# State tiles two items ahead, sums between the first products, and scratch in the other PSUM banks

## The chip, the cores and the metric

The kernel runs on one core of one Trainium2 chip. The metric is the device time of one execution in microseconds (us). All arithmetic is in float32; the large products use the float32r form of TensorE's input, in three matmuls each (hi x hi, hi x lo, lo x hi).

Names used below: PE is TensorE (matmul), DVE is VectorE, ACT is ScalarE, POOL is GpSimd, and SP is SyncE, which here only issues DMAs. POOL issues DMAs too. Each engine works through its own queue in order, and so do the two queues that issue DMAs.

## The reference

One layer of a hybrid decoder, for a prompt of 1024 tokens and, with the same weights, one step of 8 samples. Cut to what matters:

```python
shift, scale, gate = split(silu(c) @ w_ada + b_ada, 3)
h = rmsnorm(x, g_norm) * (1 + scale) + shift
p = h @ w_in                      # 2048 -> 8200: q k v o z, gates i f, u v_cm z_cm
h_ml = mLSTM heads (4 heads of 256), chunkwise, with a state C of 256x256 per head
h_cm = u * spatial_mix(layernorm(gelu(v_cm))) * silu(z_cm)
out = concat([h_ml, h_cm]) @ w_out
y = rmsnorm(x + gate * out, g_final)
```

For the samples the state comes in and goes out: `C_new = decay * C + g_end * v k^T`, and `C q` enters the head's output. There are 8 x 4 states of 256 x 256. The outputs are y for both groups, the new states, and the normalised rows of the second branch.

## The kernel before

The kernel is traced by a planner that puts instructions into each engine's queue. It is free to move an instruction ahead of others that were written before it when it holds that one to be ready sooner; `late(...)` forbids that for one instruction: it stays behind everything already written on its engine. Tiles come from pools with a fixed number of slots for each tag; a new tile waits until the slot's last reader is done.

**Stages.** First x is loaded and its row norms are taken (lines 1346 to 1365). The squares are summed through `accum_out`; their element results go to a PSUM tile `tr` that nobody reads. PSUM has two tags of four banks: `pp` (`psb()`, general use) and `px` (`psx()`, the large products). Then `ada_first` computes shift and scale of the first 512 features (L197 loads, L201 matmuls, L204 a copy).

`sub_phase` computes p = h @ w_in with a seven-product scheme (Strassen's), in three passes over the inner dimension (`SUBS`): 32 sections of 256 output columns each, and for each section seven products (`product`, L387) of a weight combination (`sums` L360, `split` L371/L372) with one of seven combinations of h. These seven combinations for each block of 256 features are made by `combos`: for each an ACT cast (L310) and a DVE subtraction (L311), and four more DVE operations (L316, L317, L323, L330), 11 DVE operations a block. `combos` is a generator of seven steps. The first pass takes blocks 0 and 1. Before it, for each of the two, `h_block` makes h (transposes L276, ACT L277, gate product L283) in the one tile `hf` of pool `pre` (one slot), and `combos` then runs to its end. `bg` is the background of a pass: one of its steps after each product. In the first pass it begins with `ada_pair` for blocks 2 to 4 (weight loads L174 on SP, three slots; matmuls L178), whose copy takes a scratch tile of tag `s2` (three slots). `combos` takes three such tiles a block, and `sample_two` (L422) one for each pair of sections, stored through SP.

After the third pass and the streams that compute the heads, `out_proj` multiplies by w_out: two halves of the tokens, four column groups each, 16 tiles k of w_out in a group. For each k, `take` loads tiles of w_out through SP five ahead (lines 887 to 889) and has ACT cast (L870) and DVE subtract (L871) three ahead; then come 12 matmuls (L908, L909, L910). From the second group on, the sample's work `back_b` runs between them: after 14 of the 16 tiles of a group one step, after every second of these one more, which is 21 steps a group.

**The sample's steps.** `s_sum` and `s_ml1` prepare sums, gates and scaled rows (18 steps). Then come the 16 state items `s_state(b, hp)`: POOL loads a state tile `Ct` (L1190, 128 x 1024, 512 KB) and two tiles of q and k rows spread over all partitions (`g2`, L1194, 256 KB each); ACT scales the tile (L1198, twice), DVE multiplies it with q (L1202, four times) and adds the new part (L1207, four times); POOL stores it (L1210). `Ct` has three slots (`CTB`), `g2` four in all. In each round of two steps one item is loaded, the item before it is computed, and the item before that is stored. All of these are `late`.

After that `s_cm` and `s_ml2` finish both branches of the sample with small transfers, and `s_out` multiplies by w_out again: 32 loads of 512 KB on POOL into the same `Ct` slots, issued two ahead (L1262), each with four matmuls (L1294), and a final norm.

Of the kernel before, what the change touches and what calls it, by code (L numbers as in the profile page):

```python
# [8 lines left out]
F32 = mybir.dt.float32  # L9
# [5 lines left out]
P = 128  # L15
# [3 lines left out]
NB = 8  # L19
# [14 lines left out]
def tile_decoder_step(  # L34
# [26 lines left out]
    def nm(s):  # L61
        uid[0] += 1
        return f"{s}{uid[0]}"
# [25 lines left out]
    def psb():  # L89
        return pp.tile([P, 512], F32, tag="pp", name=nm("pp_"))  # L90
# [335 lines left out]
        A.copy(e, ps)  # L426
        to_dram(sa.sub, psd[:, sa.n * 256:sa.n * 256 + 512], e)

    def sub_phase(sub, at, bg, turn=None):
        secs = {}  # L430

        def get(n):
            if n < len(SECS) and n not in secs:
                secs[n] = Seven(sub, n)

        AHEAD = 2
        get(0)
        get(1)
        secs[0].sums()
        for m in range(AHEAD):  # L440
            secs[0].split(m)
        last = len(SECS) - 1
        for n in range(len(SECS)):
            s = secs[n]
            s.load_co()
            if n == last and turn is not None:
                for _ in bg:
                    pass
                bg = turn()
            for m in range(7):  # L450
                if m == 3 and n + 1 < len(SECS):
                    secs[n + 1].sums()
                g = m + AHEAD
                if g < 7:
                    s.split(g)
                elif n + 1 < len(SECS):
                    secs[n + 1].split(g - 7)
                if m == 1 and n % 2 == 0:
                    sample_two(s, secs[n + 1])
                s.product(m, at)  # L460
                for _ in range(1 if sub < 2 else (0, 2, 0, 2, 0, 0, 3)[m]):
                    next(bg, None)
            s.store()
            if sub == len(SUBS) - 1 and n:
                avail.add(SECS[n - 1])
            get(n + 2)
            del secs[n]
        avail.update(SECS if sub == len(SUBS) - 1 else [])
        if turn is not None:
            for _ in bg:  # L470
                pass
# [738 lines left out]
        late(G.dma_start(nC_s[0, b, 2 * hp_:2 * hp_ + 2].rearrange("h (a p) d -> p (h a) d", p=P), Ct))  # L1210
        yield

    CTB = 3

    def s_ml2(so):
        d, v, cq = sv["d"], sv["v"], sv["cq"]
# [29 lines left out]
    def s_out():  # L1246
        ts_ = []
        for _ in range(4):
            yield
        for n in range(4):  # L1250
            t = g2([NB, 512])
            late(G.dma_start(t, hc_d[:, n * 512:n * 512 + 512]))
            ts_.append(t)
        rows = [(n, hf, kq) for n in range(4) for hf in range(2) for kq in range(4)]
        raws = {}

        def get(i):
            if i < len(rows) and i not in raws:
                n, hf, kq = rows[i]
                raws[i] = pl["wp"].tile([P, 4, 256], F32, tag="Ct", name=nm("Ct"), bufs=CTB)  # L1260
                c0 = n * 512 + hf * 256
                late(G.dma_start(raws[i], wout[:, 4 * kq:4 * kq + 4, c0:c0 + 256]))  # L1262

        for i in range(CTB - 1):
            get(i)
        for _ in range(4):
            yield
        pt = psb()
        for n in range(4):
            for i in range(4):  # L1270
                kt = 4 * n + i
                late(T.transpose(pt[:, kt * NB:kt * NB + NB], ts_[n][:, i * P:i * P + P], ident[0:NB, 0:NB]))
        V.tensor_copy(hs[:, :, 0:NB], pt[:, 0:KT * NB].rearrange("p (k b) -> p k b", b=NB))
        yield
        part = sm([NB, 4])
        ys = []
        pend = None

        def row(n, e, xl, gt):
            p2 = psb()  # L1280
            late(T.matmul(p2[0:16, :], sel9, e, start=True, stop=True))
            y = pl["gp"].tile([NB, 512], F32, tag="ym"[n // 2], name=nm("ys"), bufs=2)
            V.tensor_tensor(out=y, in0=p2[0:NB, :], in1=gt, op=ALU.mult)
            V.tensor_tensor(out=y, in0=y, in1=xl, op=ALU.add)
            t = g2([NB, 512])
            A.activation(t, y, AF.Square, accum_out=part[:, n:n + 1])
            ys.append(y)

        for i, (n, hf, kq) in enumerate(rows):
            if (hf, kq) == (0, 0):  # L1290
                ps = psb()
            raw = raws.pop(i)
            for g in range(4):
                late(T.matmul(ps[32 * g:32 * g + 32, hf * 256:hf * 256 + 256], hs[:, 4 * kq + g, :], raw[:, g, :],  # L1294
                              start=(kq == 0), stop=(kq == 3), tile_position=(0, 32 * g)))
            get(i + CTB - 1)
            if (hf, kq) == (0, 1) and pend is not None:
                row(*pend)
                pend = None
            if (hf, kq) == (1, 3):  # L1300
                e = g2([P, 512])
                A.copy(e, ps)
                xl = pl["wp"].tile([NB, 512], F32, tag="gt", name=nm("xl"), bufs=4)
                late(G.dma_start(xl, x_sample[:, 0, n * 512:n * 512 + 512]))
                gt = pl["wp"].tile([NB, 512], F32, tag="gt", name=nm("gt"), bufs=4)
                late(G.dma_start(gt, gate_d[0:NB, n * 512:n * 512 + 512]))
                pend = (n, e, xl, gt)
            yield
        yield
        row(*pend)  # L1310
        ssq, rs = sm([NB, 1]), sm([NB, 1])
        V.tensor_reduce(out=ssq, in_=part, axis=AX.X, op=ALU.add)
        G.tensor_scalar(out=rs, in0=ssq, scalar1=1.0 / DM, scalar2=EPS, op0=ALU.mult, op1=ALU.add)
        G.tensor_tensor(out=rs, in0=rs, in1=mhalf[0:NB, 0:1], op=ALU.pow)
        for n in range(4):
            gt = pl["wp"].tile([NB, 512], F32, tag="gt", name=nm("gt"), bufs=4)
            late(G.dma_start(gt, gfin[:, n * 512:n * 512 + 512].partition_broadcast(NB)))
            yield
            V.scalar_tensor_tensor(out=ys[n], in0=ys[n], scalar=rs, in1=gt, op0=ALU.mult, op1=ALU.mult)
            G.dma_start(y_sample[:, 0, n * 512:n * 512 + 512], ys[n])  # L1320


    def back_b():
        so, decb = sv["so"]
        yield from s_sum()
        yield from s_ml1(so)
        g0 = g1 = iter(())
        for b in range(NB + 1):
            for hp_ in range(2):
                g2_ = s_state(b, hp_, decb) if b < NB else iter(())  # L1330
                next(g2_, None)
                yield
                next(g1, None)
                next(g1, None)
                next(g0, None)
                g0, g1 = g1, g2_
                yield
        yield from s_cm()
        yield from s_ml2(so)
        yield from s_out()  # L1340
# [5 lines left out]
    for tt in range(8):  # L1346
        part_ = sm([P, 4])
        xr = [pl["s1"].tile([P, 2, 512], F32, tag="asS", name=nm("xr"), bufs=7) for _ in range(2)]
        for n in range(4):
            if n % 2 == 0:  # L1350
                S.dma_start(xr[n // 2].rearrange("p a b -> p (a b)"), xp[:, tt, n * 512:n * 512 + 1024])
            tr = psb()
            xv = xr[n // 2][:, n % 2, :]
            if n % 2 == 0:
                A.activation(tr, xv, AF.Square, accum_out=part_[:, n:n + 1])
            else:
                V.scalar_tensor_tensor(out=tr, in0=xv, scalar=1.0, in1=xv, op0=ALU.mult, op1=ALU.mult, accum_out=part_[:, n:n + 1])
# [12 lines left out]
    def hf_tile(pool="pre"):  # L1370
        t = pl[pool].tile([P, 4, 512], F32, tag="hf", name=nm("hf"), bufs=1)
        return t, [t[:, i, :] for i in range(4)]

    sets = [("as", "A"), ("as", "B"), ("as", "C"), ("s1", "S")]
    at = {b: [] for b in range(8)}
    ada_first()
    for blk in range(2):
        hf = hf_tile()[1]
        for _ in h_block(blk, lambda tt: xk[tt // 2][:, tt % 2, blk * 256:blk * 256 + 256], [0, 1], hf):
            pass  # L1380
        for _ in combos(at[blk], sets[blk], hf, V):
            pass

    nxt = {}

# [32 lines left out]
    def turn_b():  # L1418
        close_pool("adp")
        open_pool("hf2", "right")  # L1420
        t, hf = hf_tile("hf2")
        S.dma_start(t.rearrange("p a b -> p (a b)"), hf7)
        g6, g7 = combos(at[6], sets[2], nxt[6][1], V), combos(at[7], sets[0], hf, V)
        for _ in range(7):
            next(g6)
            next(g7)
            yield

    sub_phase(0, [at[0], at[1]], bg_a(), turn_a)
    sub_phase(1, [at[2], at[3], at[4]], bg_b(), turn_b)  # L1430
    for name in ("hf2", "pre", "co"):
        close_pool(name)
# [20 lines left out]
    open_pool("w2", "right")  # L1453

    def turn():
        close_pool("co")
        close_pool("c2")
        open_pool("ya", "left")
        open_pool("wp", "left")

    out_proj(streams, turn, back_b())
    for name in ("wp", "ya", "rp", "gp", "w2", "hx"):
        close_pool(name)
# [29 lines left out]
```

## Time and profile before

| | us |
|---|---|
| median of 3 runs | 2180.51 |
| lowest and highest | 2178.35, 2185.18 |
| profiled execution | 2184.66 |
| its span, from first to last instruction | 2182.9 |

| engine | busy us | share of the span |
|---|---|---|
| PE (matmul) | 2010.4 | 92% |
| PE weight load | 1511.3 | 69% |
| DVE | 1344.2 | 62% |
| ACT | 856.4 | 39% |
| POOL | 321.0 | 15% |

The core moved 402.68 MB by DMA, 184 GB/s over the span; the mean granted clock of PE was 0.969 of full speed. In the chain of work that ended last, the largest DMA part is the store of state tiles (out_dram<-Ct, 3% of the span).

How to read it: matmuls are pipelined and their ends are modelled, so a busy PE can still be short of its peak; the granted clock tells how fast it was let run. A share of busy time is a mean over stages with different limits, which is why the stretches are looked at one by one. Releasers of waits are inferred from semaphore events.

### The profile page before, as it was taken

What the parts mean: (1) busy time and instruction counts of PE and PEld (TensorE: products, weight loads), DVE (VectorE), ACT (ScalarE), POOL (GpSimd) and SP (SyncE); (2) the same over time, 40 slices, a digit from 0 to 9 for tenths busy, and PEclk for the clock granted to TensorE, in tenths of its full rate; (3) what the DMA queues carried; (4) which work ended last, traced back from release to release, by engine and by line L of the source; (5) the groups of instructions that cost most, each with busy time, mean ns of one, the idle gap of its engine ahead of it and who ended that gap; (6) DMA issues with size and microseconds to landing.
All of it is one profiled execution on the core that took longest, in us unless ns stands there. A gap on an engine that the chain in (4) does not pass through costs nothing. (4 is left out here: it accounts for less than half of the span.)

```text
span 2182.9 us, 29261 instructions
## 1 busy us (share of the span) xinstructions
PE 2010.4 (92%) x10175; PEld 1511.3 (69%) x10175; DVE 1344.2 (62%) x2775; ACT 856.4 (39%) x1771; POOL 321.0 (15%) x499
## 2 busy tenths in 40 slices
PE   2999999999999999998899999999998996767997
PEld 1467777766766777777688788788786775554476
DVE  3568777755644555558667767767766655453264
ACT  2435434433422233334346456456455433231132
POOL 1000000011111111111211111111110132244300
PEclk9999999999999999999999999999999998878999
DMA  8685444488799676665676776776877877867843
GB/s 282 205 281 182 174 160 172 175 231 214 179 247 241 124 136 127 129 128 114 141 176 138 166 194 138 181 181 138 181 165 174 261 209 207 237 203 249 275 132 134
DMA packets 227396, 402.68 MB, mean 184 GB/s; under 512 B 20784, under 2 KB 136192, under 8 KB 226984
## 3 DMA queue, kind: packets, MB, share of 16 engines
q1 hardware_dynamic: 188560, 280.92, 40.4%
q0 software_dynamic: 38688, 119.89, 28.7%
q8 instruction: 80, 1.31, 0.3%
q14 instruction: 68, 0.56, 0.1%
HBM read 259.56 MB, written 141.19 MB: 184 GB/s over the span
## 5 line engine op out<-in xcount | busy, mean ns | idle before, releaser
L387 PE MATMUL px<-as,hi 128*128 128x512 f32 x3584 | 1147.5, 401 | 17.6 <-DVE pu L390 8.3
L387 PEld LDWEIGHTS px<-as,hi 128*128 128x128 f32 x3584 | 660.6, 189 | 214.9 <-issue 25.9
L387 PE MATMUL px<-as,lo 128*128 128x512 f32 x1792 | 707.5, 396 | 2.4 <-DVE lo L372 2.2
L387 PEld LDWEIGHTS px<-as,lo 128*128 128x128 f32 x1792 | 338.7, 189 | 82.6 <-DVE lo L372 4.4
L371 ACT CAST hi<-t 128x384 fp32r<-128x384 f32 (+1 forms) x384 | 182.5, 477 | 397.9 <-PE px L387 390.7
L372 DVE TENSOR_TENSOR lo<-t,hi 128x384 fp32r<-128x384 f32 (+1 forms) x384 | 195.4, 509 | 161.5 <-ACT hi L371 161.3
L371 ACT CAST hi<-raw 128x384 fp32r<-128x384 f32 (+1 forms) x288 | 137.3, 477 | 370.4 <-PE px L387 336.9
L908 PE MATMUL px<-whi,hx 128*128 128x512 f32 x512 | 212.8, 418 | 31.7 <-DVE yacc L993 22.2
L910 PE MATMUL px<-wlo,hx 128*128 128x512 f32 x512 | 212.0, 419 | 29.8 <-DVE wlo L871 29.8
L336 POOL DMA_DIRECT2D spool<-co x128 | 112.1, 876 | 809.0 <-DVE co L390 567.5
L909 PE MATMUL px<-whi,hx 128*128 128x512 f32 x512 | 210.5, 412 | 1.1 <-DVE hx L902 1.1
L372 DVE TENSOR_TENSOR lo<-raw,hi 128x384 fp32r<-128x384 f32 (+1 forms) x288 | 146.5, 509 | 50.8 <-ACT hi L371 50.3
L908 PEld LDWEIGHTS px<-whi,hx 128*128 128x128 f32 x512 | 102.2, 200 | 63.4 <-issue 18.0
L910 PEld LDWEIGHTS px<-wlo,hx 128*128 128x128 f32 x512 | 103.0, 202 | 61.0 <-DVE wlo L871 35.1
L870 ACT CAST whi<-raw 128x512 fp32r<-128x512 f32 x128 | 77.1, 617 | 172.0 <-PE px L909 132.8
L390 DVE TENSOR_TENSOR co<-pa,px 128x512 f32<-128x512 f32 x192 | 129.1, 683 | 24.8 <-PE px L387 24.5
L871 DVE TENSOR_TENSOR wlo<-raw,whi 128x512 fp32r<-128x512 f32 x128 | 85.1, 686 | 85.3 <-ACT whi L870 74.5
L909 PEld LDWEIGHTS px<-whi,hx 128*128 128x128 f32 x512 | 102.4, 200 | 26.0 <-issue 3.7
L390 DVE TENSOR_TENSOR co<-pu,px 128x512 f32<-128x512 f32 x96 | 65.8, 686 | 88.3 <-PE px L387 88.3
L390 DVE TENSOR_TENSOR pa<-pa,px 128x512 f32<-128x512 f32 x96 | 65.8, 686 | 76.8 <-PE px L387 76.4
L360 DVE TENSOR_TENSOR t<-raw 128x768 f32<-128x768 f32 (+1 forms) x96 | 83.3, 868 | 12.5 <-DMA raw<-in_w_in_dram 9.9
L390 DVE TENSOR_TENSOR pu<-pa,px 128x512 f32<-128x512 f32 x96 | 65.6, 683 | 38.6 <-PE px L387 36.5
(359 smaller groups left out, 1983.5 us busy)
## 6 DMA issues: line engine op xcount, KB each, us to landing
spool<-co POOLq DMA_DIRECT2D x128, 512.0 KB, 6.4
raw<-in_w_in_dram SPq DMA_DIRECT2D x64, 768.0 KB
ad<-in_w_ada_dram SPq DMA_DIRECT2D x88, 512.0 KB
spool<-co SPq DMA_DIRECT2D x64, 512.0 KB
raw<-in_w_out_dram SPq DMA_DIRECT2D x128, 256.0 KB
im<-spool SPq DMA_DIRECT2D x40, 512.0 KB
raw<-in_w_in_dram SPq DMA_DIRECT2D x32, 512.0 KB
Ct<-in_w_out_dram POOLq DMA_DIRECT2D x32, 512.0 KB, 5.9
```

The source lines that it names most:

```text
L336: G.dma_start(out, t, accum_op=ALU.add)
L360: sub = lambda o, a, b: V.tensor_tensor(out=o, in0=a, in1=b, op=ALU.subtract)
L371: A.copy(hi, w)
L372: V.tensor_tensor(out=lo, in0=w, in1=hi.bitcast(F32), op=ALU.subtract)
L387: T.matmul(o, w[:, b, :], at[b][m][:, d, :], start=(first and b == 0 and n == 0), stop=(b == nb - 1 and n == 2), skip_group_check=True)
L390: add = lambda o, a, b, op=ALU.add: V.tensor_tensor(out=o, in0=a, in1=b, op=op)
L870: A.copy(hi, raw)
L871: V.tensor_tensor(out=lo, in0=raw, in1=hi.bitcast(F32), op=ALU.subtract)
L908: T.matmul(po, h[:, k, 0, tk], hi, start=first, stop=False)
L909: T.matmul(po, h[:, k, 1, tk], hi, start=False, stop=False)
L910: T.matmul(po, h[:, k, 0, tk], lo, start=False, stop=last)
```

## The change

1. In `out_proj`, when the streams are done, the pools `gp` (rows) and `rp` (small scratch) are closed and opened again with eight slots of `g2` and seven of `r1`.
2. `Ct` has five slots instead of three. The items are loaded two ahead: two loads come first, then each round of three steps loads item i+2, takes the ACT and first DVE part of item i, and then the second DVE part of item i and the store of item i-1. `s_out` loads four ahead, as its depth is `CTB - 1`.
3. In `s_out` the rows `y`, `xl` and `gt` come from `g2` instead of tags of their own or of the foreground's pool.
4. The h of block 1 gets two tiles of the pool of x instead of the one slot of `hf`; `h_block` runs for both blocks, and the `combos` of the two run side by side, one step of each before each of the first section's seven products.
5. The scratch of the squares (`tr`) takes the banks of `px` instead of `pp`.

```diff
-    def sub_phase(sub, at, bg, turn=None):
+    def sub_phase(sub, at, bg, turn=None, first=iter(())):
...
+                next(first, None)
                 s.product(m, at)
...
-    CTB = 3
+    CTB = 5
...
-            y = pl["gp"].tile([NB, 512], F32, tag="ym"[n // 2], name=nm("ys"), bufs=2)
+            y = g2([NB, 512])
...
-                xl = pl["wp"].tile([NB, 512], F32, tag="gt", name=nm("xl"), bufs=4)
+                xl = g2([NB, 512])
...
-                gt = pl["wp"].tile([NB, 512], F32, tag="gt", name=nm("gt"), bufs=4)
+                gt = g2([NB, 512])
...
-        g0 = g1 = iter(())
-        for b in range(NB + 1):
-            for hp_ in range(2):
-                g2_ = s_state(b, hp_, decb) if b < NB else iter(())
-                next(g2_, None)
-                yield
-                next(g1, None)
-                next(g1, None)
-                next(g0, None)
-                g0, g1 = g1, g2_
-                yield
+        items = [s_state(b, hp_, decb) for b in range(NB) for hp_ in range(2)]
+        for i in range(2):
+            next(items[i])
+            yield
+        for i in range(len(items) + 1):
+            if i + 2 < len(items):
+                next(items[i + 2])
+            yield
+            if i < len(items):
+                next(items[i])
+            yield
+            if i < len(items):
+                next(items[i])
+            if i:
+                next(items[i - 1])
+            yield
...
-            tr = psb()
+            tr = psx()
...
+    hf0 = [hf_tile()[1], []]
+    for _ in range(2):
+        t = pl["s1"].tile([P, 2, 512], F32, tag="asS", name=nm("hf"), bufs=7)
+        hf0[1] += [t[:, 0, :], t[:, 1, :]]
     for blk in range(2):
-        hf = hf_tile()[1]
-        for _ in h_block(blk, lambda tt: xk[tt // 2][:, tt % 2, blk * 256:blk * 256 + 256], [0, 1], hf):
+        for _ in h_block(blk, lambda tt: xk[tt // 2][:, tt % 2, blk * 256:blk * 256 + 256], [0, 1], hf0[blk]):
             pass
-        for _ in combos(at[blk], sets[blk], hf, V):
-            pass
+
+    def both(a, b):
+        for _ in range(7):
+            next(a)
+            next(b)
+            yield
...
-    sub_phase(0, [at[0], at[1]], bg_a(), turn_a)
+        yield from both(combos(at[6], sets[2], nxt[6][1], V), combos(at[7], sets[0], hf, V))
+
+    sub_phase(0, [at[0], at[1]], bg_a(), turn_a, both(*(combos(at[i], sets[i], hf0[i], V) for i in range(2))))
...
     def turn():
-        close_pool("co")
-        close_pool("c2")
+        for name in ("co", "c2", "rp", "gp"):
+            close_pool(name)
+        open_pool("gp", "left", GB)
+        open_pool("rp", "left", 7)
         open_pool("ya", "left")
         open_pool("wp", "left")
 
+    GB = 8
```

## Rows read from the trace of the kernel before

**Rows 1.** The page: busy time, share and instructions.

```profile
PE 2010.4 (92%) x10175; PEld 1511.3 (69%) x10175; DVE 1344.2 (62%) x2775; ACT 856.4 (39%) x1771; POOL 321.0 (15%) x499
```

**Rows 2.** Stretches: us, PE, PEld, DVE, ACT, POOL busy (count), clock, DMA share, GB/s.

```profile
1759.00:1940.00 181.00, 130.15 (x475) 100.00 (x474) 96.23 (x270) 58.77 (x111) 46.99 (x65) 0.84 0.79 231
1990.00:2083.00 93.00, 83.23 (x487) 47.55 (x487) 28.55 (x45) 19.57 (x42) 29.43 (x42) 0.94 0.79 256
2083.00:2167.00 84.00, 84.00 (x374) 68.25 (x374) 41.55 (x65) 22.39 (x43) 4.83 (x10) 1.00 0.39 106
1710.00:1740.00 30.00, 26.66 (x108) 20.89 (x107) 19.81 (x35) 9.87 (x21) 1.09 (x2) 0.94 0.85 278
```

**Rows 3.** The same view, two slices of 10 us among the state items.

```profile
1770.00:1780.00 10.00, 10.00 (x46) 8.29 (x45) 9.93 (x31) 8.39 (x18) 2.18 (x3) 1.00 0.99 316
1890.00:1900.00 10.00, 7.06 (x17) 5.28 (x18) 5.69 (x18) 2.86 (x5) 2.91 (x4) 0.66 0.74 172
```

**Rows 4.** The chain that ended last, 1797 to 1810: start, length, what.

```profile
1797.49 0.49 POOL Ct L1190
...
1799.64 8.98 DMA out_dram<-Ct
...
1809.18 0.49 POOL Ct L1190
```

**Rows 5.** By line: landing times of L1190, then L1194, then L1210.

```profile
DMA to landing us min/median/max: 4.2/5.7/14.4
...
DMA to landing us min/median/max: 5.7/7.5/13.0
...
DMA to landing us min/median/max: 7.0/8.8/11.9
```

**Rows 6.** Groups, 1759 to 1940: count, busy us, mean ns, idle before and releasers.

```profile
L1202 DVE SCALAR_TENSOR_TENSOR r<-Ct,g 128x256 f32<-128x256 f32 x64 | 23.4, 421 | 70.2 <-DMA g<-psa 64.6 <-ACT hx L901 5.6
...
L1194 POOL DMA_DIRECT2D g<-psa x32 | 22.7, 713 | 12.7 <-DVE r L1202 11.3 <-DVE Ct L1207 0.9 <-DVE hx L902 0.5
...
L870 ACT CAST whi<-raw 128x512 fp32r<-128x512 f32 x39 | 22.6, 613 | 10.1 <-PE px L909 8.8 <-ACT Ct L1198 0.8 <-ACT whi L870 0.6
...
L1198 ACT ACTIVATE Ct<-Ct,decb 128x512 f32<-128x512 f32 x32 | 21.4, 714 | 90.5 <-DMA Ct<-in_state_C_dram 90.5
...
L1190 POOL DMA_DIRECT2D Ct<-in_state_C_dram x16 | 12.1, 757 | 112.4 <-DMA out_dram<-Ct 103.8 <-issue 8.5
```

**Rows 7.** The same view, 1990 to 2083.

```profile
L908 PE MATMUL px<-whi,hx 128*128 128x512 f32 x72 | 31.7, 440 | 0.0
...
L1262 POOL DMA_DIRECT2D Ct<-in_w_out_dram x32 | 24.3, 761 | 53.4 <-PE pp L1294 48.4 <-DMA Ct<-in_w_out_dram 2.4 <-PE px L910 2.1
...
L1294 PE MATMUL pp<-Ct,hs 128*32 128x256 f32 x248 | 19.9, 398 | 9.4 <-DMA Ct<-in_w_out_dram 9.2
```

**Rows 8.** By line, L1262: issue ns min/median/max, first and last start.

```profile
L1262 POOL DMA_DIRECT2D Ct<-in_w_out_dram x32: 751/751/807, 1990.9 to 2071.0; - x32
```

**Rows 9.** Instructions in order of time, 40 to 80: start, length, idle before.

```profile
40.99 1.07 PE L201 MATMUL pp<-ad,scT 128*32 128x512 f32 x2 [20.33 <-DVE pp L1357]
...
57.99 31.65 SPq L174 DMA_DIRECT2D ad<-in_w_ada_dram  x8
...
64.40 2.79 ACT L277 ACTIVATE hf<-pp,shf,scl 128x512 f32<-128x512 f32 x4 [1.98 <-DVE hs L219]
...
76.29 0.68 DVE L330 TENSOR_TENSOR s<-hf,s 128x512 f32<-128x512 f32 x1
...
77.53 2.78 ACT L277 ACTIVATE hf<-pp,shf,scl 128x512 f32<-128x512 f32 x4
```

**Rows 10.** Stretches at the start, columns as in Rows 2.

```profile
32.00:66.00 34.00, 21.42 (x98) 7.87 (x100) 9.31 (x29) 6.52 (x16) 2.97 (x8) 0.91 1.03 364
68.00:82.00 14.00, 10.90 (x58) 5.46 (x58) 8.50 (x15) 7.12 (x13) 0.00 (x0) 0.88 0.00 0
66.00:90.00 24.00, 20.55 (x111) 9.29 (x110) 16.76 (x30) 14.32 (x28) 0.00 (x0) 0.91 0.30 95
```

More of the change, by code (lines that the diff above doesn't have):

```diff
@@ L1315, in s_out @@
         for n in range(4):
-            gt = pl["wp"].tile([NB, 512], F32, tag="gt", name=nm("gt"), bufs=4)
+            gt = g2([NB, 512])
             late(G.dma_start(gt, gfin[:, n * 512:n * 512 + 512].partition_broadcast(NB)))
@@ L1422, in turn_b @@
         S.dma_start(t.rearrange("p a b -> p (a b)"), hf7)
[L1423 to L1427, printed above, removed]
-    sub_phase(0, [at[0], at[1]], bg_a(), turn_a)
+        yield from both(combos(at[6], sets[2], nxt[6][1], V), combos(at[7], sets[0], hf, V))
+    sub_phase(0, [at[0], at[1]], bg_a(), turn_a, both(*(combos(at[i], sets[i], hf0[i], V) for i in range(2))))
     sub_phase(1, [at[2], at[3], at[4]], bg_b(), turn_b)
```

## The prediction

> **What bounds the kernel now.** I read the page first, then busy time by stretch, then the chain of waits of the stretch that looked worst, then who waited there and what each transfer took.
>
> The page has PE busy 92% of the span [rows 1]. A PE that counts as busy at a lower clock hides more, so the end is read by stretch [rows 2]. From 2083 to 2167 PE is full at clock 1.00 and passes 374 matmuls, nearly all of 512 columns, in 84 us: 0.225 us each. In the stretch of the state items (1759 to 1940, 181 us) it is busy 130 us at a mean clock of 0.84; but the 475 matmuls recorded there are only 475 x 0.225 = 107 us of work, so 74 us are stall and slow clock. From 1990 to 2083, where the sample's output product runs, three groups of 72 or 73 matmuls (L908 stands for them) are 217 x 0.225 = 49 us and L1294 is 20 us [rows 7]: 69 us of work in 93.
>
> The chain of waits says why in the first of these [rows 4]. It runs along POOL's queue: a load of a state tile (L1190), two row loads (L1194), a store (L1210), then nothing until that store has landed, then the next load; from 1797.5 to 1809.2, 11.7 us for one item. A store lands in 8.8 us at the median, a load in 5.7, a row load in 7.5 [rows 5]. The groups of the stretch say the same from the other side [rows 6]: POOL sat idle 103.8 us for stores, and because the tiles come late, ACT sat 90.5 us for state tiles and DVE 64.6 us for rows. ACT and DVE also make the hi and lo parts of the weights, in the same queues, so PE stands behind them.
>
> **The change, part by part.** The sums are made against the profiled execution, 2184.7 us (its span is 2182.9). The median of the runs shown is 2180.5, 4.2 us less; the same gain is subtracted from it.
>
> *State items.* The slot that item i's load needs was item i-3's and becomes item i-5's. On POOL the order is now load i+2, store i-1, load i+3, and this last one needs store i-2, issued a whole period before. So the 8.8 us of a store leave the chain as long as a period is longer than what is left of its landing. POOL's own issue work stays: 0.76 for the load, twice 0.71 for the rows [rows 6], and a store's taken as a load's, 2.9 us an item, so it is not the next limit. The rows take two tiles an item, and eight in the new pool last for four items; behind a load that still waits stand the next two row loads and one store. What is late next is the transfers themselves. The stretch moved 231 GB/s x 181 us = 41.8 MB at a DMA share of 0.79 [rows 2], and about the same bytes must pass in the new one: by the new program the items take 53 steps instead of 36, which at 21 steps for a block of 16 weight tiles are 40 tiles, and the old stretch really passed 39 (L870) [rows 6]. Equal work, then, and the question is the rate. Bounds: 231 GB/s as now, no gain; 316 GB/s, the best 10 us of this stretch, at share 0.99 [rows 3], 132 us, -49. The 30 us from 1710, where transfers of this kind were queued, had 278 at 0.85 [rows 2]; that is the nearest row. I take 275, since loads, stores and small row reads are mixed: 41.8 / 275 = 152 us, **-29 us**.
>
> The Trainium skill (DMA: Bandwidth & Descriptors, Specifications) gives the 16 DMA engines a ceiling of 435 GB/s. By that figure the 41.8 MB would be 96 us, PE would be the bound, and this stretch would gain over 70 us. The slice of 316 GB/s at share 0.99 [rows 3] speaks against it for this mix; a faster one is among the rivals, priced from rows.
>
> *1940 to 1990.* Small dependent transfers one behind another, which the change leaves as they are; one scratch tile fewer (seven for eight) is not missed, as no item keeps more than four. 0.
>
> *Output product of the sample.* Five slots let four loads fly instead of two. The 32 loads are issued from 1990.9 to 2071.0, 2.6 us apart [rows 8], and POOL sits 48.4 us until PE gives a slot back [rows 7]. Four in flight would halve the distance, and then bytes decide: 256 GB/s x 93 us = 23.8 MB [rows 2]. At 280, a little above the row of 278 as these are mostly loads, it is 85 us: **-8 us**. Bounds: 0 as now, and PE's 69 us, -24. The sample, gate and gain rows that move to the row pool free slots of the foreground's pool and cost nothing where they go: eight tiles hold four results and the four others of one row. With 17 more steps ahead of it the sample's end moves from the last block but one into the start of the last; about 11 tiles, 25 us of PE's time. Now PE is busy for 84 us behind it [rows 2], which covers that; without this cover each us of it would count.
>
> *Start.* Before, block 1's four ACT passes (L277) wait for the only tile of h, which block 0's last sum (L330, at 76.3) frees: they start at 77.5, where block 0's ended at 67.2 [rows 9]. With tiles of their own they follow at once, and so do block 1's sums and its first product. Two things limit the gain. DVE: the two blocks' 22 operations of 0.68 us (as L330) are 15 us, and it was idle for 7.2 of the 24 us from 66 to 90 [rows 10], so at most that goes. DMA: nothing moved from 68 to 82 [rows 10], because SP's queue stood 31.65 us on eight weight loads (L174) [rows 9] that wait for slots which PE frees late; an earlier PE ends this hole earlier. I take **-5 us**. Bounds: -9, and +5, since two sets of interleaved sums want six of three scratch tiles, and the sample's first product keeps one until a store queued on SP behind those eight loads has landed.
>
> *PSUM scratch.* PE waited for the squares' scratch until 41.0 (L201, 20.33 us) [rows 9], but from 32 to 66 the DMA was at a share of 1.03 [rows 10], so the weights would come no sooner. 0; bounds -2 and 0. The banks it moves to are free until the first products.
>
> Sum: -29 - 8 - 5 = **-42 us**: 2142.7 for a profiled execution, 2138.5 as a median.
>
> **The rivals.**
> *Transfers are the bound already.* For it: a slice of the stretch with 172 GB/s at share 0.74 [rows 3], 232 at full share. Against it: its mean is 231 / 0.79 = 292. If only 245 is reached, the stretch takes 171 us, -10, the rest -2: 2168.
> *Transfers are no bound, PE is.* The start moved 364 GB/s for 34 us [rows 10]. With that the stretch takes 115 us by bytes, close to PE's 107, -66; the product PE's 69, -24; the start -5: 2180.5 - 95 = 2085. Against it: those are weights and inputs in long rows, and the stretch itself never passed 316.
> *The change doesn't do what it says.* The planner's order or the reopened pools put the store that was just issued before the next load again; then only the start moves: 2176.
> *Slower: the foreground's weight tiles starve.* SP loads five tiles of w_out ahead (line 887), through the same DMA engines. With more of POOL's transfers in flight each of them takes longer. Now a tile passes every 181 / 39 = 4.6 us; five are 23 us, so from a landing of 23 us on the stretch is longer than before. At 26 us it is 5.2 us a tile, 208 us for 40, +27, less 13 elsewhere: 2195. Against it: the worst load of a state tile, when the first three items and their rows were in flight together, landed in 14.4 us [rows 5].
>
> **How the numbers follow.** The forecast's own range takes the rate from 255 to 316 GB/s (-17 to -49), the product 0 to -18, the start +4 to -9: 2105 to 2168, with a chance of 0.68. Transfers bound already 0.13, PE the bound 0.07, no effect 0.05, starving 0.07. Eight times in ten: 2100 to 2170. This kernel can be told from no change at about 0.3%, 6.5 us. Faster: 0.68 + 0.07 + 0.11 of the first rival = 0.86; within: 0.02 of it and no effect, 0.07; slower: 0.07.
>
> **What would show it.** Right: POOL's idle time before L1190 falls from 103.8 us to under 30; the items' loads come about 9 us apart; the stretch's DMA share is near 0.9 and its clock above 0.84; L1262 comes less than 2.6 us apart; block 1's L277 follows block 0's, and the hole from 68 to 82 is shorter. Wrong: a period of the items still above 11 us; a shorter period with a weight tile still every 4.6 us, PE then being held by something else; or a first section of products that ends later than now.

## The result, and the profile after

The changed kernel takes 2121.59 us (median of 4 runs, 2120.11 to 2131.19), the kernel before 2182.85 in the same comparison (4 runs): a ratio of 0.973 with a 95% interval of 0.9695 to 0.9765, so 61 us faster. 2138.5 was predicted, within 2100 to 2170. The direction, the range and the mechanism of the state items held; the gain came out half as large again as forecast, and not all in the places that were named.

The page's first part, after (busy time, share, instructions; against [rows 1]):

```profile
PE 1993.4 (94%) x10175; PEld 1500.8 (71%) x10175; DVE 1342.5 (63%) x2775; ACT 857.9 (40%) x1771; POOL 320.1 (15%) x499
```

The counts are those of before: nothing was taken out, so all of the gain is stall and slow clock. (From line 460 to the code of the items' round, a line of the changed kernel has a number one higher: L1190 is now L1191.)

To see where it came from, both spans are cut at the ends of the output projection's blocks, that is where VectorE has done the fourth L993 (after: L994) of a block. Busy time by stretch, blocks (0,2), (0,3), (1,0), (1,1) and (1,2), columns as in [rows 2]; first the kernel before:

```profile
1773.00:1846.00 73.00, 52.71 (x201) 41.38 (x200) 39.51 (x122) 22.23 (x42) 19.66 (x27) 0.85 0.73 220
1846.00:1929.00 83.00, 56.90 (x199) 42.91 (x198) 43.64 (x121) 27.32 (x52) 19.73 (x28) 0.83 0.80 235
1929.00:1999.00 70.00, 53.20 (x197) 40.93 (x196) 36.94 (x76) 18.15 (x39) 36.52 (x67) 0.79 0.66 209
1999.00:2082.00 83.00, 73.58 (x453) 40.97 (x451) 23.92 (x38) 16.81 (x34) 25.62 (x36) 0.98 0.82 263
2082.00:2127.00 45.00, 45.00 (x201) 35.64 (x200) 26.13 (x42) 13.34 (x27) 5.36 (x11) 1.00 0.49 134
```

The same blocks after:

```profile
1765.00:1814.00 49.00, 47.19 (x203) 37.24 (x202) 36.97 (x110) 21.93 (x41) 18.20 (x25) 1.00 1.01 327
1814.00:1892.00 78.00, 55.41 (x196) 42.15 (x195) 45.04 (x124) 29.41 (x54) 17.42 (x24) 0.85 0.85 261
1892.00:1945.00 53.00, 45.85 (x192) 36.37 (x191) 38.96 (x87) 18.17 (x40) 30.02 (x59) 0.94 0.76 249
1945.00:2001.00 56.00, 56.00 (x320) 39.69 (x319) 19.59 (x32) 13.38 (x28) 17.92 (x27) 0.97 0.89 278
2001.00:2063.00 62.00, 60.27 (x349) 39.74 (x347) 26.72 (x43) 16.90 (x35) 15.26 (x22) 1.00 0.68 212
```

With the ends to a tenth of a us (before 1773.1, 1929.2, 1998.8, 2127.0; after 1765.5, 1892.2, 1945.0, 2063.4) the books are:

| part | before | after | change | predicted |
|---|---|---|---|---|
| start to the end of (0,1) | 1773.1 | 1765.5 | -7.6 | -5 |
| (0,2) and (0,3): the items | 156.1 | 126.7 | -29.4 | -29 |
| (1,0): last items, small transfers, first of the product | 69.6 | 52.8 | -16.8 | 0 |
| (1,1) and (1,2): the sample's product | 128.2 | 118.4 | -9.8 | -8 |
| the rest, to the last matmul | 42.4 | 42.8 | +0.4 | 0 |

The sum is -63.2 (the span went from 2182.9 to 2119.3). Three of the terms look close, and block (1,0), which was costed at nothing, is the second largest. But the blocks are not the stretches that the prediction priced: before, block (1,0) holds the last 11 us of the items and the first 9 us of the product beside the 50 us of small transfers. So the same is told once more by the prediction's own stretches. The small transfers, before and after, then the items' last 11 us before:

```profile
1940.00:1990.00 50.00, 38.00 (x147) 30.41 (x147) 27.60 (x53) 10.94 (x23) 31.17 (x61) 0.86 0.63 201
1908.00:1952.00 44.00, 36.85 (x145) 28.74 (x144) 27.42 (x52) 13.79 (x31) 26.71 (x55) 0.88 0.68 220
```

```profile
1929.00:1940.00 11.00, 6.54 (x17) 4.42 (x16) 5.70 (x18) 4.74 (x10) 2.07 (x3) 0.66 0.85 267
```

The output product after, 1952 to 2042 (three lines of 97 matmuls like the first; before in [rows 7]):

```profile
L909 PE MATMUL px<-whi,hx 128*128 128x512 f32 x97 | 40.3, 416 | 0.0
...
L1295 PE MATMUL pp<-Ct,hs 128*32 128x256 f32 x240 | 17.7, 387 | 0.0
```

Taking off 0.225 us for each matmul of 512 columns and the product's own time, as the prediction did, leaves what each stretch loses to waits and to a slow clock (estimates, since matmuls at an edge count on both sides):

| stretch | length before, after | lost before, after | change of what is lost | predicted |
|---|---|---|---|---|
| the items | 181, 157 | 74, 38 | -36 | -29 |
| the small transfers | 50, 44 | 17, 11 | -6 | 0 |
| the sample's product | 93, 90 | 24, 7 | -17 | -8 |

Besides, the items begin 8.6 us earlier (-5 was predicted). The product's stretch is hardly shorter, but 291 foreground matmuls pass in it where 217 did, so less is left behind it. By this count the product was forecast 9 us too small, the items 7 and the small transfers 6.

The signs that the prediction named, in the profile after. First the stretch of the items by its own ends, the stretch of the output product, one slice of 10 us and the hole of the start:

```profile
1751.00:1908.00 157.00, 132.61 (x529) 103.92 (x528) 105.11 (x285) 61.97 (x116) 50.45 (x72) 0.92 0.91 283
1952.00:2042.00 90.00, 90.00 (x553) 60.02 (x552) 30.09 (x47) 21.81 (x42) 27.84 (x40) 1.00 0.91 289
1780.00:1790.00 10.00, 10.00 (x44) 7.64 (x43) 2.85 (x11) 2.48 (x4) 3.37 (x5) 1.00 1.01 349
68.00:82.00 14.00, 11.37 (x80) 5.29 (x78) 9.87 (x18) 6.87 (x14) 0.00 (x0) 0.88 0.64 198
```

The item stretch runs at a share of 0.91 (0.79 in [rows 2]) and a clock of 0.92 (0.84); its items follow each other in 8.92 us, not 10.77 (from the first L1208 of the first item to the first of the last, a fifteenth; L1207 before). The hole at the start is 0.64 full, not 0.00 [rows 10].

The load of the state tile by its line: count and first and last start, what POOL's idle time before it ended on, and the landing time:

```profile
L1191 POOL DMA_DIRECT2D Ct<-in_state_C_dram x16: 748/748/830, 1750.8 to 1868.3; - x16
...
  DMA out_dram<-Ct: 27.8, 7
...
DMA to landing us min/median/max: 4.4/9.4/16.4
```

POOL's wait for stores fell from 103.8 us [rows 6] to 27.8, under the 30 that was asked for. The median landing of a load rose from 5.7 us [rows 5] to 9.4, and the second item in hand pays for it.

Who waits in the item stretch now (us, times, longest):

```profile
ACT hx L902 <- DMA hr<-hcd: 42.3, 10, 15.3
POOL out_dram L1211 <- DVE Ct L1208: 33.1, 6, 9.7
...
POOL Ct L1191 <- DMA out_dram<-Ct: 27.8, 7, 6.3
```

ACT's 90.5 us for state tiles and DVE's 64.6 for rows [rows 6] are gone: L1199 and L1203 have no idle time before them. In their place stands a wait that the prediction did not have: `hr<-hcd`, the input tiles of the second half, which SP loads in block (0,3) into two slots, each asked for only when the subtraction (L903) that reads the last but one is done. The chain that ended last, 1836 to 1876:

```profile
1842.83 6.70 DMA hr<-hcd
...
1850.98 10.34 DMA hr<-hcd
...
1862.78 8.96 DMA hr<-hcd
```

At a DMA share of 0.85 in this block these landings take 7 to 10 us, and each stands between two casts. That this is why (0,3) went only from 83 to 78 us, while (0,2) went from 73 to 49, is tested below.

### The profile page after: what moved, and what is told of

It is laid out like the page before. It is cut to its first block, busy times and chain, and to the rows that moved or that the text cites. A ratio compares the mean times of both kernels' runs of the same rounds, so it can differ in the third digit from the quotient of the medians.

```text
span 2119.3 us, 29251 instructions
## 1 busy us (share of the span) xinstructions
PE 1993.4 (94%) x10175; PEld 1500.8 (71%) x10175; DVE 1342.5 (63%) x2775; ACT 857.9 (40%) x1771; POOL 320.1 (15%) x499
## 5 line engine op out<-in xcount | busy, mean ns | idle before, releaser
L909 PE MATMUL px<-whi,hx 128*128 128x512 f32 x512 | 210.4, 413 | 31.9 <-ACT whi L871 16.8
L911 PE MATMUL px<-wlo,hx 128*128 128x512 f32 x512 | 206.3, 405 | 4.8 <-DVE wlo L872 4.7
L910 PE MATMUL px<-whi,hx 128*128 128x512 f32 x512 | 205.5, 402 | 1.1 <-DVE hx L903 1.1
L909 PEld LDWEIGHTS px<-whi,hx 128*128 128x128 f32 x512 | 100.0, 195 | 69.2 <-ACT whi L871 23.2
L872 DVE TENSOR_TENSOR wlo<-raw,whi 128x512 fp32r<-128x512 f32 x128 | 86.7, 687 | 94.8 <-ACT whi L871 93.0
L871 ACT CAST whi<-raw 128x512 fp32r<-128x512 f32 x128 | 78.1, 617 | 165.2 <-PE px L910 128.8
L911 PEld LDWEIGHTS px<-wlo,hx 128*128 128x128 f32 x512 | 99.5, 195 | 30.1 <-DVE wlo L872 8.7
L910 PEld LDWEIGHTS px<-whi,hx 128*128 128x128 f32 x512 | 100.2, 196 | 21.5 <-DVE hx L903 1.7
```

The costliest lines, as they stand in the source:

```text
L871: A.copy(hi, raw)
L872: V.tensor_tensor(out=lo, in0=raw, in1=hi.bitcast(F32), op=ALU.subtract)
L909: T.matmul(po, h[:, k, 0, tk], hi, start=first, stop=False)
L910: T.matmul(po, h[:, k, 1, tk], hi, start=False, stop=False)
L911: T.matmul(po, h[:, k, 0, tk], lo, start=False, stop=last)
```

## The experiments

Theory A, formed from these traces: the items were held by the store in POOL's chain; without it the bytes of the stretch bound it; the start edits do little. Against it stood that the distance of two items, rather than the store, makes the gain; that latency or the plan's steps, not bytes, set the new pace; and that the start edits give the 5 us.

"Blocks" below is the time from the end of (0,1) to the end of (1,2), 353.9 us before and 297.9 after; it leaves out what the start does. Kernels that differ in the start alone differ in it too: 353.9, 357.3 and 361.0 with the items of before, 297.9, 300.2 and 304.4 with those of the change. Differences below some 7 us are not read from it.

**The squares' scratch alone** (the kernel before with one edit):

```diff
-            tr = psb()
+            tr = psx()
```

> The kernel before with only the squares' scratch moved to the px banks. Theory A (scratch frees the first weight products): in the changed kernel the first shift and scale (L217) came at 59.9 instead of 63.7 and its first products waited less; so alone it gains 3 to 5 us, 2178 to 2180 beside a before of 2182.9, and L217 lies near 60. Rival B (as predicted, the DMA holds the weights): L217 stays at 63 to 64 and the time within 1 us of before.

2182.03 us, ratio 0.9988 (0.9973 to 1.0003). The shift rows (L217) are ready at 59.9, not 63.7; the first section of products ends at 91.0 (94.6) and the passes at 1649.9 (1653.7). So a term that was costed at 0 gives 3.8 us as far as 1650. At the end of the kernel the times cannot tell it from nothing, and so cannot decide between the theories: in this profile block (0,3) ends 1.9 us earlier, and the last matmul 1.3 later than before.

**The interleaved sums alone** (the kernel before, with block 1's tile of h and `both(...)` between the products):

```diff
...
-    sub_phase(0, [at[0], at[1]], bg_a(), turn_a)
+    sub_phase(0, [at[0], at[1]], bg_a(), turn_a, both(*(combos(at[i], sets[i], hf0[i], V) for i in range(2))))
```

> The kernel before with only the sums of the first two blocks between the first section's products (own tiles for block 1's h, the two generators side by side). Theory A: the sums side by side lack scratch (three tiles for six), block 1's last hi/lo operation (L311) ends some 4 to 5 us later than it could, so alone this loses 0 to 4 us or gains nothing, and the changed kernel's start owes its gain to the PSUM scratch. Rival B (as predicted): alone it gains about 5 us, first section's end (L404) some 5 us earlier than 94.6.

2184.06 us, ratio 0.9997 (0.9984 to 1.0011): nothing. The last of the 14 sums ends at 98.8 (90.6 before) and the first section at 96.4 (94.6). The -5 of the prediction did not come from this edit.

**The items without both start edits:**

> The changed kernel without the two changes at the start: five slots, two items ahead, reopened pools, rows of the last product from the row pool. Theory A: it carries nearly all of the 61 us, 55 to 60: 2123 to 2128. Rival B: the start shifts the phase of everything behind it and the parts do not add; then under 50 us, above 2133.

2126.67 us, ratio 0.9731 (0.971 to 0.9752), the changed kernel's own ratio; blocks 300.2 us. All of the gain that the times can resolve is the part of the items and the product; the intervals leave room for some us of the start.

**Four slots instead of five:**

```diff
-    CTB = 5
+    CTB = 4
```

> The changed kernel with four slots of the state tile instead of five; the order of issue is the same, so load i+3 needs the store i-1 that stands right before it in POOL's queue. Theory A (the gain is the store that leaves the chain): the period of the items goes back to a store's landing plus the issues, 11 to 14 us, POOL waits over 100 us for stores, and 25 us or more of the gain are lost, 2147 or above. Rival B (the gain is the distance of two items between load and use): the period stays below 10 us and the time within 8 us of the changed kernel, 2122 to 2130.

2137.36 us, ratio 0.9782 (0.976 to 0.9804), which is what neither theory said. Who waited, 1746 to 1918:

```profile
POOL Ct L1191 <- DMA out_dram<-Ct: 102.5, 12, 11.9
ACT Ct L1199 <- DMA Ct<-in_state_C_dram: 51.1, 9, 8.3
```

The store is back in POOL's chain, with a wait as long as before (103.8 us), and the two item blocks take 140.2 us (156.1 before, 126.7 after). What is shorter than before is ACT's wait for the tiles, 51.1 us for 90.5; the distance of two items, the fourth slot and the eight row slots came together here, and which of them did it is not shown.

**The old round with five slots, and with four:**

```diff
-        items = [s_state(b, hp_, decb) for b in range(NB) for hp_ in range(2)]
...
+        g0 = g1 = iter(())
+        for b in range(NB + 1):
+            for hp_ in range(2):
...
-    CTB = 5
+    CTB = 4
```

> The changed kernel with its five slots and reopened pools, but with the kernel before's round of two steps an item: the state tile is loaded one item ahead of its decay, not two. Theory A (the distance of two items is worth the most, since with four slots only about 16 of the 61 us went): ACT and VectorE wait for the state tile again (over 30 us each in block (0,3)), the period is 10 us or more and the time 2145 or more. Theory B (slots free of the store are worth the most): the wait of GpSimd for the stores stays under 40 us, the period under 9.6 and the time at 2135 or less.

> The kernel of the old round (one item ahead) with four slots instead of five. Here the store that a load waits for was issued one round before, as in the changed kernel, but the load is one item ahead, not two; four slots with the new round had the store just ahead of the load. Theory A (a load is free once the store it waits for is one round old; the distance adds nothing then): 2117 to 2128, GpSimd's wait for the stores under 40 us. Theory B (four slots are too few whatever the round): 2134 or more, GpSimd's wait 80 us or more.

Five slots: 2121.16 us, ratio 0.9704 (0.9679 to 0.9728); four: 2123.45, ratio 0.9716 (0.9695 to 0.9737). Both are the changed kernel's time, so the new round is not needed for it. Who waited in the one with four, 1748 to 1900:

```profile
POOL Ct L1191 <- DMA out_dram<-Ct: 36.7, 10, 6.1
ACT Ct L1199 <- DMA Ct<-in_state_C_dram: 35.0, 8, 7.8
```

What counts is the age of the store that a load waits for. In the old round with three slots (the kernel before) and in the new round with four, it was issued just ahead of the load: 2183 and 2137 us. In the old round with four and the new round with five it is one round old: 2123 and 2122. With five in the old round it is two rounds old: no load waits for a store there any more, and nothing more comes: 2121. Four slots instead of five change the store's age and the product's loads (three ahead, not four); the two rounds with four slots differ in the age too, and by 14 us. The eight row slots are in all of these kernels and were not varied alone; before, POOL stood 12.7 us ahead of row loads, most of it for a row slot [rows 6]. One thing did not go as expected: with the old round the items follow each other in 7.11 us, faster than the 8.92 of the new one, and ACT still waits 35 to 38 us for state tiles; yet the time is the same. The stretch of the items with five slots and the old round:

```profile
1743.00:1870.00 127.00, 94.49 (x372) 74.71 (x372) 80.66 (x244) 46.47 (x86) 47.03 (x65) 0.88 0.94 289
```

It is 30 us shorter than after, but 372 matmuls were recorded in it, not 529, at the same rate of bytes: what the items gain, the weights lose.

**Fewer bytes:**

```diff
+    rows_ = {}
...
-        qb, kb = g2([P, 512]), g2([P, 512])
-        for t, key in ((qb, "q"), (kb, "k")):
+        n = 2 * b + hp_
+        if n < 4:
+            rows_[n] = [g2([P, 512]), g2([P, 512])]
+        qb, kb = rows_[n % 4]
+        for t, key in ((qb, "q"), (kb, "k")) if n < 4 else ():
```

> The changed kernel, with the q and k rows of the first four items alone loaded; the other twelve items use those again, so 12 x 0.52 MB of broadcast loads are left out and the states come out from the wrong rows. Theory A (bytes bound block (0,2) and (0,3) now: share 0.91, 283 GB/s over 157 us): 6.3 of 44.4 MB go, 14%, so the stretch falls by 15 to 22 us to about 138 and the time to 2100 to 2107. Theory B (the loads' latency and the plan's three steps an item bound it): the stretch stays within 6 us of 157, its share falls to some 0.78, and the time is 2115 or more.

2097.11 us, ratio 0.9601 (0.9578 to 0.9623), 24 us less than after; the blocks take 273.7 us, also 24 less. Stretch and waits:

```profile
1751.00:1890.00 139.00, 130.75 (x554) 105.94 (x552) 110.68 (x295) 64.57 (x121) 33.77 (x52) 0.96 0.90 294
```

```profile
ACT whi L871 <- PE px L910: 29.4, 14, 3.9
ACT hx L902 <- DMA hr<-hcd: 20.1, 8, 4.8
```

The rate stays (294 GB/s at 0.90 for 283 at 0.91), the time falls with the bytes, and PE is busy 131 of 139 us. So bytes cost time in the changed kernel's stretch, some 24 / 6.3 = 3.8 us per MB, until PE is full. That bytes alone bound it is not shown: ACT's wait for `hr` fell from 42.3 to 20.1 us in the same run.

**Seven scratch tiles for the sums** (`s2`, three before):

> The changed kernel with seven scratch tiles instead of three for the sums of the blocks, so that no sum waits for the scratch that the sample's store or its neighbour holds. Theory A (the shortage of scratch took back what the interleaving won): the last sum of block 1 ends at 91 us or before, not at 96.0, the first section's copy at 91 or before (93.6), the passes end 2 to 4 us earlier; at the end of the kernel 0 to 3 us, 2118 to 2122. Theory B (VectorE's order and its casts hold the sums): the last sum ends at 95 or later and the time does not change.

2126.46 us, ratio 0.9713 (0.969 to 0.9736): no gain, and the last sum ends at 95.5. (That end alone would decide nothing: in the other kernels with both start edits and three tiles it lies between 93.0 and 96.3.) The wait of a sum for its scratch is gone, but VectorE, whose queue is in order, now stands longer on a product whose result it has to add ahead of the sums; VectorE, 81 us:

```profile
81.31 0.69 DVE L390 TENSOR_TENSOR pu<-pa,px 128x512 f32<-128x512 f32 x1 [3.57 <-PE px L387]
```

In the changed kernel the wait there is for the scratch (the block of h's own passes first, ACT, then VectorE):

```profile
60.31 2.78 ACT L277 ACTIVATE hf<-pp,shf,scl 128x512 f32<-128x512 f32 x4 [1.68 <-DVE scl L216]
64.70 0.78 ACT L277 ACTIVATE hf<-pp,shf,scl 128x512 f32<-128x512 f32 x1 [1.62 <-PE pp L276]
```

```profile
59.90 0.18 DVE L217 TENSOR_TENSOR shf<-pp,pfm 128x36 f32<-128x36 f32 x1
...
78.01 0.69 DVE L316 TENSOR_TENSOR s<-hf,hf 128x512 f32<-128x512 f32 x1 [2.00 <-DMA psd<-s]
```

**The second half's input tiles asked for three ahead** (four `hr` slots; to make room the weight tiles' `raw` slots go from six to four, in a second kernel to five, and there the gate's `gt` from four to three):

```diff
...
+                        if i == 0:
+                            for k_ in KORD[:HRB - 1]:
+                                hr_get(1, k_)
+                        if i + HRB - 1 < KT:
+                            hr_get(1, KORD[i + HRB - 1])
                         hx_load(1, k)
```

> The changed kernel with the second half's input tiles (the loads hr<-hcd of block (0,3)) asked for three ahead in four slots instead of two, and the weight tiles' raw slots cut from six to four to make the room. Theory A (these loads are late because they are asked for one step before their cast): ACT's wait for hr falls from 42.3 to under 15 us, the stretch of the items from 157 to 148 or less, the time to 2105 to 2114. Theory B (the transfers are at their bound, whatever is asked for first): ACT's wait moves to the weight tiles or the state tiles, the stretch stays at 153 or more and the time at 2118 or more.

> The changed kernel with the second half's input tiles three ahead in four slots, the weight tiles' raw slots five instead of six and the gate's slots three instead of four. Theory A (with four raw slots ACT waited 58.2 us for weight tiles since they were asked for late): the wait falls to 40 us or less and the time to 2098 to 2105. Theory B (the transfers' bytes are the bound, a fifth slot asks earlier and gets it no sooner): the wait stays at 50 us or more, the time within 2105 to 2112.

With four raw slots 2108.42 us, ratio 0.9643 (0.9618 to 0.9669); with five 2102.95, ratio 0.9636 (0.9613 to 0.9659). Both beat the changed kernel, and cannot be told apart. Who waited in the first, 1748 to 1905 (L871 is the weights' cast, L911 the input tiles'):

```profile
ACT whi L871 <- DMA raw<-in_w_out_dram: 58.2, 19, 9.8
...
ACT hx L911 <- DMA hr<-hcd: 9.1, 6, 2.7
```

In the second, 1748 to 1900:

```profile
ACT whi L871 <- DMA raw<-in_w_out_dram: 31.5, 9, 7.7
...
ACT hx L911 <- DMA hr<-hcd: 23.0, 11, 6.2
```

Theory A of the first had the time and the wait for `hr` right; theory B had right where ACT's wait went, to the weight tiles, but not that the time stays. With five raw slots the wait for them is 31.5 us, so part of the 58.2 came from the slots that were given away. In the second kernel, theory A had both the wait and the time right. A wait for weight tiles costs less, presumably since three pairs of weights are made ahead; no run shows that alone. Block (0,3) takes 63.2 and 65.6 us (78.7 after), and in the second, 1810 to 1875, the transfers run at 0.92 where the changed kernel's (0,3) had 0.85:

```profile
1810.00:1875.00 65.00, 52.03 (x198) 39.85 (x196) 45.42 (x124) 30.00 (x55) 17.46 (x24) 0.89 0.92 299
```

So the changed kernel's transfers were not yet at a bound there: the late `hr` tiles held them. They cost some 13 to 19 us by the medians, 10 to 14 by the blocks (288.3 and 284.1 us).

**The same with the old round** (four raw slots):

> The old round with five slots, and the second half's input tiles asked for three ahead in four slots (weight tiles' raw slots four, not six). Theory A (the two gains stand beside each other, since either way the same bytes go in the stretch and PE is the bound behind it): 2103 to 2113, as with the new round (2108.4). Theory B (items at some 7 us a piece take the transfers from the weight tiles, with two raw slots fewer): 2116 or more, and block (0,2) ends 10 us or more later against its start than with the new round (55.3 us).

2120.14 us, ratio 0.9708 (0.969 to 0.9725), blocks 297.5: theory B. Here the new round earns its place: its three steps an item hold the items back (8.40 us with four raw slots against 6.73), and block (0,2) takes 55.3 us with it, 67.7 with the old round. That the weights gain the transfers which the items leave is the reading of this; no run paced the items alone.

**State tiles of the first four items ahead of the sample's row work** (on the kernel with five raw slots):

```diff
...
         yield from s_sum()
+        for i in range(4):
+            ct_load(i // 2, i % 2)
         yield from s_ml1(so)
```

> The kernel with the second half's input tiles three ahead, five raw slots and three gate slots (2102.95 us), and the state tiles of the first four items loaded ahead of the sample's row work instead of behind it: 2.1 MB in a stretch of 14 us that ran at a DMA share of 0.40. Theory A (bytes bound the items' stretch; leaving 6.3 MB out took 24 us, 3.8 us per MB): up to 8 us less, 2094 to 2100. Theory B (the first items wait for the rows or for the plan's steps, and the small loads of the row work, now behind four 512 KB transfers, make the items start later): the first decay is no earlier and the time is 2101 to 2106.

2106.24 us (5 runs, 2095.01 to 2110.25), ratio 0.9633 (0.9608 to 0.9658): not to be told from the kernel without it, as theory B had it. The two stretches that the loads were moved into, and the one behind:

```profile
1717.00:1730.00 13.00, 13.00 (x60) 10.74 (x59) 4.56 (x8) 2.71 (x5) 6.81 (x12) 1.00 0.99 326
1730.00:1744.00 14.00, 13.98 (x62) 11.25 (x60) 6.03 (x19) 3.33 (x6) 8.60 (x17) 1.00 0.49 128
1744.00:1760.00 16.00, 13.30 (x52) 10.77 (x53) 8.51 (x19) 6.00 (x15) 5.15 (x8) 0.89 0.95 155
```

The second of them without the early loads:

```profile
1730.00:1744.00 14.00, 14.00 (x64) 11.58 (x62) 6.03 (x19) 3.38 (x6) 10.68 (x22) 1.00 0.40 96
```

The stretch at 0.40 became 0.49 only: the loads start at 1719.9, where the engines were at 0.93 already, and the small transfers behind them come later. Blocks 281.3 us, 2.8 less, which is within their spread.

## Why the prediction was right, and where it was not

**State items, -29.** Right in mechanism: the store's age decides, as the sum had it. The size was near, but that the two blocks give -29.4 is partly luck. The stretch became 24 us shorter, not 29, and yet loses 36 us less, as more of the foreground passed in it. The rate was well taken (283 GB/s where 275 were taken), and bytes cost time next, as the sum had it. Two things compensated. The stretch moved 157 x 283 = 44.4 MB, not 41.8, since 44 weight tiles passed, not 40. And (0,3) was held by `hr` tiles. This is the rival of the starving foreground in a small form: not the five weight tiles, whose raw wait was 12.8 us, but the one load in the foreground that was asked for one step ahead; it took some 10 to 19 us back, and the stretch did not become longer, as it would have by that rival.

**The term that was put at nothing: "1940 to 1990 ... which the change leaves as they are", 0.** It lost some 6 us less (17 to 11). Block (1,0), 16.8 us shorter, is more than this term: by estimate some 7 us of it are the end of the items, which before lay in this block at a clock of 0.66, and some 4 lie in the first 9 us of the product. The transfers are indeed the same. VectorE's wait for one of them (L1231, after L1232) is even longer after. What was not priced is who stands behind that wait. VectorE and then PE, before, 1971:

```profile
1971.25 0.41 DVE L1231 TENSOR_TENSOR r<-r,sr 32x256 f32<-32x256 f32 x1 [4.29 <-DMA r<-cq_d]
```

```profile
1972.98 2.07 PE L910 MATMUL px<-wlo,hx 128*128 128x512 f32 x4 [8.64 <-DVE wlo L871]
```

The same after, 1935:

```profile
1935.41 0.41 DVE L1232 TENSOR_TENSOR r<-r,sr 32x256 f32<-32x256 f32 x1 [5.12 <-DMA r<-cq_d]
```

```profile
1937.18 0.47 PE L909 MATMUL px<-whi,hx 128*128 128x512 f32 x1 [2.07 <-ACT sr L1233]
```

Before, seven products of the first half's scaling (L931, 4.71 us) ran just ahead of the wait, and the low parts of the weights (L871) stood behind both, so PE ran dry for 8.64 us; the 10 us from 1970 had a mean granted clock of 0.59, near the lower of its two levels (1.2 of 2.4 GHz). After, two low parts (L872, from 1929.02) run just ahead of the same wait and PE loses 2.07. In sum PE's idle time in the block fell from 16.8 us to 7.2 and its busy time from 53.2 to 45.9 (197 and 192 matmuls, clock 0.79 and 0.94). That these two alignments make the 6 us of the term is read from one profile of each kernel; no run moved the scaling alone. That (1,0) is shorter is no accident of one profile: it takes 68.8 to 69.7 us in the three kernels with the items of before and 51.5 to 57.0 in the eight with the new round; with the old round and more slots it takes 62.5 to 63.8 us, with part of the product already in it.

**The term that was too small: output product, -8.** The step that failed is "then bytes decide". The blocks' -9.8 looks near, but the stretch itself lost some 17 us less. L1263 comes every 2.69 us, not under 2.6, though four loads fly: with the tiles there in time PE no longer waits for them (0.0 before L1295, 9.4 us before L1294 in [rows 7]), fills the stretch with foreground matmuls and is itself what holds the loads back. PE's 90.00 busy of 90 us, and POOL's wait for it, show this:

```profile
  PE pp L1295: 52.8, 17
...
DMA to landing us min/median/max: 4.1/6.4/11.0
```

PE, not bytes, bounds it now, near the lower end (-24) that the prediction kept as a bound. The gain shows as matmuls in the same stretch: 553 recorded in 90 us, where [rows 2] have 487 in 93. The product's loads at two ahead, with the rest as changed, were not tried.

**Start, -5, and scratch, 0.** The two were exchanged, as far as the profiles show: the scratch gives 3.8 us by 1650, the sums nothing. The bound of +5 for the sums had the mechanism (scratch held by a store, 2.00 us at 78.01), but taking it away did not help, since products stand in VectorE's queue in its place. Of the -7.6 at the end of (0,1) the runs confirm a part: the three kernels without the scratch edit end their passes at 1652 to 1657 us, the eleven with it at 1642 to 1650, which differ among themselves by 8 us, and the ratios do not show it.

**The rivals.** "Transfers are the bound already" was wrong by its rate (245 against 283), yet right that bytes come next. "PE is the bound" was wrong for the items, where PE was busy 132.61 of 157 us, and right for the product. The Trainium skill's ceiling of 435 GB/s (DMA: Bandwidth & Descriptors, Specifications) stays out of reach for this mix: at shares of 0.97 to 1.02 the slices show 318 to 349.

## What to carry to other kernels

Where loads and stores share slots on an in-order queue, count how long ago the store was issued that each load waits for: one round of age freed the queue here whether it came from a fourth slot or from a fifth with a longer look ahead, and a second round of age gave nothing. Near full transfers, the tile that is asked for latest pays: here two slots of a foreground input cost 10 to 19 us. Price a background stretch by the foreground work that it lets pass, not by its length: the product's stretch became 3 us shorter and was worth some 17. And a stretch that "does not change" still has to be priced by what it will stand next to: in these two profiles the same wait on an in-order queue cost PE 8.6 us or 2.1, by what had been made before it.

## What was not expected of the hardware

Items at 7.1 us or at 8.9 us each gave the same time (2121.16 and 2121.59): at a DMA share over 0.9 (289 and 283 GB/s) the faster items came with slower weights (372 matmuls in 127 us, 529 in 157). Rate at full share depends on the mix: 349 GB/s in 1780 to 1790, 327 over (0,2), and 155 at a share of 0.95 in 1744 to 1760 of the last kernel.
